# Two partial-sum buffers from the pooling path, and three operands loaded in place, in the last projection

## The chip, the core and the metric

The kernel runs on one core of one Trainium2 chip. The metric is the device time of one execution in microseconds (us). TensorE is called PE in the profile, VectorE DVE, ScalarE ACT, GpSimd POOL and SyncE SP; DMA transfers are issued by SP, in order, and each issue may first wait for semaphores. A wait at the head of SP's queue holds up every transfer that stands behind it.

## The reference, cut to what matters

Two layers work on 1024 latent tokens of 1024 channels (and 256 context tokens). The even layer runs a convolution branch and a gated linear recurrence side by side; the odd layer pools over windows, gates and projects back. The change touches only the end of the odd layer and the residual sum behind it:

```
z = h @ p["w_in"]
u, g = jnp.split(z, [W_POOL], axis=-1)
d = multiscale_pool(...)            # windows 2, 4, 8, 16 along rows of 64 tokens
y = einsum(d, w_grp) * scale
out = (y * silu(g)) @ p["w_out"]    # 2048 -> 1024 channels: the last projection
x = x + gate * out
return rmsnorm(x, final_g)
```

## The kernel before

Activations lie channels by tokens: a tile is 128 channels on the partitions by 1024 tokens, or one of its halves of 512. Products are taken in three passes for precision: each float32 operand is split into a high and a low part (`split`, lines 101 to 103: ACT casts the high part, DVE subtracts it for the low part), and PE multiplies high by high, high by low and low by high (`prod`, lines 931, 933 and 934). On top of this the large products use a Strassen-like scheme on 2 by 2 blocks with seven products: `quad` takes weights p1 to p7 and seven operands b11, t1, t2, b21, t3, b22 and t4, and sums into three PSUM tiles named qa, qb and qc. There are four PSUM tiles of 512 columns for this (`pm`), so the next quad can begin while one tile of the last one is still in use.

The last projection has 2048 input channels. It is computed in two halves of 1024 (part 0, names ending in `wo0`; part 1, `wo1`), and each half in four quads for the output rows m, m+1 with m = 0, 2, 4, 6. The last two quads of part 1 are written out apart (`last_half0`, names ending in `_l`). In the profile the buffer numbers are left out: `qa_wo`, `y_t3h`, `wq_wo` stand for all quads and both parts, and `h` and `l` at the end of an operand are its high and low part.

- **Operands.** The seven operands of each part lie in DRAM (`y_raw`). `y_operand` loads each as two tiles of 128 by 1024 into a raw tile (`yr_t...`, `yr_b...`, line 1350), and splits it into a high and a low tile. For b11, b21 and t4 these lie in `dpool`, for t1, t2, t3 and b22 in `d2pool`, which has 16 tiles: exactly the four such operands of one part, so that those of part 1 take over the tiles of part 0. The raw tiles come from `xpool` (8 tiles). For part 1, t3, b22 and t4 are loaded one after the other in the first quad of part 1 (line 1516), and use few raw tiles in turn.
- **Weights.** `wquad` loads two raw tiles (`wr_wo`, line 897; two buffers in all, so that the next quad's weights can be loaded only when the split of this quad's is through) and makes the seven weights (`ws_wo`, `wr_wo` sums at lines 911 to 919, `wq_wo` splits).
- **Partial sums.** For each quad of part 0, `put` loads a half row of the residual stream that the first layer left in DRAM (`xp` from `x1_part`, line 1472), adds the PSUM result times the gate (`gated`, line 1455, DVE) and stores it back (line 1481). The tile for it comes from `vpool`, which has two buffers of 512 columns. Each quad needs four such tiles: rows i = 0 and 1, halves h = 0 and 1. In part 1 the sums are loaded whole (`x` from `x1_part`, line 1503) and end in the final norm.
- **Two other buffers.** `apool` has two buffers of 640 columns (`atile`). The pooling path uses them for window sums; from the first quad of part 1 on they hold the two running sums of squares of the final norm (`fin`).
- **y sums.** `y_sums` (lines 883 to 886 in `block_sums`) forms the operands of part 1 from the last pair of rows, with a temporary tile `yt` from `vpool`, and stores them (line 1331). It is called within `put`.

A scheduler orders the instructions of each engine from the program and its own estimates, so that a change of buffers moves instructions on all of them.

Of the kernel before, what the change touches and what calls it, by code (L numbers as in the profile page):

```python
# [9 lines left out]
F32 = mybir.dt.float32  # L10
# [6 lines left out]
S = 1024  # L17
# [4 lines left out]
H = 512  # L22
# [29 lines left out]
BOPS = ("b11", "t1", "t2", "b21", "t3", "b22", "t4")  # L52
# [3 lines left out]
def body(ctx, tc, xT, ctxT, cc, ccol, modT, modW, win, gw, wout, wu, grp, wg, wo1, small, edge, ident, outT):  # L56
    nc = tc.nc
# [14 lines left out]
    y_raw = [{n: dram.tile([P, 2 * S], F32, tag=f"y_{n}_{p}", name=f"y_{n}_{p}") for n in BOPS} for p in range(2)]  # L72
# [5 lines left out]
    def xtile(name, dt=F32):  # L78
        return xpool.tile([P, S], dt, tag="x", name=name)

    def ttile(name):
        return tpool.tile([P, H], F32, tag="t", name=name)

    def atile(name):
        return apool.tile([P, NR * PW], F32, tag="acc", name=name)
# [15 lines left out]
    def split(src, hi, lo, eng):  # L101
        return (nc.scalar.copy(hi, src),  # L102
                eng.tensor_tensor(out=lo, in0=src, in1=hi.bitcast(F32), op=sub))  # L103
# [194 lines left out]
    with ExitStack() as sctx:  # L298
# [12 lines left out]
        def raw_tile(name):  # L311
            tag = ("wr", "wh", "wl")[raws[0] % 3]
            raws[0] += 1
            return wpool.tile([P, D], F32, tag=tag, name=name)
# [310 lines left out]
    with ExitStack() as actx:  # L625
# [88 lines left out]
        for j in range(KT):  # L714
# [20 lines left out]
            name = "gb0" if final else f"xb{j + 1}"  # L735
# [6 lines left out]
            if state is None:  # L742
                for m in range(2 * KT, 3 * KT):
                    part = L[m % 6][:, :D]
# [20 lines left out]
            name = "gb1" if final else f"vg{j + 1}"  # L765
# [79 lines left out]
        lo = wpool.tile([P, D], F32R, tag="wl", name="wl_gb4")  # L845
# [18 lines left out]
    def vtile(name):  # L864
        return vpool.tile([P, H], F32, tag="v", name=name)
# [16 lines left out]
    def block_sums(b11, b12, b21, b22, t3, eng):  # L882
        eng.tensor_tensor(out=t3, in0=b22, in1=b12, op=sub)
        eng.tensor_tensor(out=b12, in0=b12, in1=b11, op=sub)
        eng.tensor_tensor(out=b11, in0=b22, in1=b12, op=sub)
        eng.tensor_tensor(out=b21, in0=b21, in1=b11, op=sub)
        return dict(t2=b11, t1=b12, t3=t3, t4=b21, b22=b22)
# [54 lines left out]
    def quad(w, name, ops, put, ahead=None):  # L942
        p1, p2, p3, p4, p5, p6, p7 = w
        a, c, b = psum(f"qa_{name}"), psum(f"qc_{name}"), psum(f"qb_{name}")
        prod(a, p1, ops["b11"], True, False)
        with tc.high_priority(offset=EVAC):
            evac = nc.scalar.copy(b, a)
        prod(c, p5, ops["t1"], True, False)
        with tc.high_priority(offset=EVAC):
            put(1, 1, c, 0)  # L950
        prod(b, p6, ops["t2"], False, False)
        with tc.high_priority(offset=EVAC):
            put(0, 1, b, 0)
        prod(a, p2, ops["b21"], False, True)
        with tc.high_priority(offset=EVAC):
            put(0, 0, a, None)
        w = None
        if ahead is not None:
            with tc.issue_after(evac.ins):
                w = ahead()  # L960
        prod(b, p7, ops["t3"], False, False)
        with tc.high_priority(offset=EVAC):
            put(1, 1, b, 1)
        prod(c, p3, ops["b22"], False, True)
        with tc.high_priority(offset=EVAC):
            put(0, 1, c, 1)
        prod(b, p4, ops["t4"], False, True)
        with tc.high_priority(offset=EVAC):
            put(1, 0, b, None)
        return w  # L970


    def keep_part(parts, name, i, x):
        parts[i] = ttile(f"s{i}_{name}")
        nc.scalar.copy(parts[i], x)
# [6 lines left out]
    def gated(n, between):  # L982
        th, tl = d2tile(f"ybh{n}", F32R), d2tile(f"ybl{n}", F32R)
        for h in range(2):
            y = vtile(f"yr{n}_{h}")
            nc.sync.dma_start(y, yb_raw[n][:, HALF[h]])
            vec(nc.vector.tensor_tensor, out=y, in0=y, in1=sbs[n][h], op=mult)
            cast(th[:, HALF[h]], y)
            gp(out=tl[:, HALF[h]], in0=y, in1=th[:, HALF[h]].bitcast(F32), op=sub)
            fill(between)  # L990
        bh.append(th)
        bl.append(tl)
# [277 lines left out]
    for i in range(KH):  # L1270
# [3 lines left out]
        t = block_sums(b11, b12, b21, b22, ttile(f"xt3_{i}"), nc.vector)  # L1274
# [66 lines left out]
    def y_sums(m):  # L1341
        t = block_sums(*y_blocks(m), vtile(f"yt3_{m}"), nc.vector)
        for name in ("t1", "t2", "t3", "t4"):
            y_store(m, name, t[name])

    def y_operand(ops, part, name, raw_tile, alloc):
        hi, lo = [], []
        for q in range(2):
            r = raw_tile(f"yr_{part}_{name}_{q}")
            nc.sync.dma_start(r, y_raw[part][name][:, q * S : (q + 1) * S])  # L1350
            hi.append(alloc(f"y{part}_{name}h{q}", F32R))
            lo.append(alloc(f"y{part}_{name}l{q}", F32R))
            split(r, hi[q], lo[q], nc.vector)
        halves = lambda ts: [t[:, h] for t in ts for h in HALF]
        ops[name] = halves(hi), halves(lo)
# [3 lines left out]
    def y_operands(part, raws, names=BOPS, alloc=None):  # L1359
        for name in names:  # L1360
            y_operand(yops[part], part, name, next(raws),
                      alloc or (dtile if name in ("b11", "b21", "t4") else d2tile))
# [11 lines left out]
    def wo1_weights(part, m):  # L1374
        return wquad([wo1[m + i, part] for i in range(2)], f"wo{part}_{m}", wo1_ring,
                     part == 1 and m >= KT - 4)
# [69 lines left out]
    def square_fin(m, h, cols, v):  # L1446
        first = fin[h] is None
        if first:
            fin[h] = atile(f"fin{h}")
        square_acc(fin[h][:, cols], v, first, f"fq{m}_{h}_{cols.start}")  # L1450
        if m in GAINED:
            nc.scalar.activation(v, v, AF.Identity, scale=col(O_FG + m))
# [6 lines left out]
    def copied(name, x):  # L1459
        t = ttile(f"b_{name}")  # L1460
        nc.scalar.copy(t, x)
        return t

    for m in range(0, KT, 2):
        parts = {}

        def put(i, h, x, part):
            if part == 0:
                keep_part(parts, f"wo0_{m}", i, x)
                return  # L1470
            t = vtile(f"xp{m}_{i}_{h}")
            nc.sync.dma_start(t, x1_part[m + i][:, HALF[h]])
            if part == 1:

                if i == 1:
                    x = copied(f"wo0_{m}", x)
                s = x if i == 0 else parts[i]
                nc.vector.tensor_tensor(out=s, in0=x, in1=parts[i], op=add)
                x = s
            gated(m + i, t, x)  # L1480
            nc.sync.dma_start(x1_part[m + i][:, HALF[h]], t)
            if (m, i, h) == (0, 0, 1):
                y_sums(NK - 2)
        def nxt():
            if m < KT - 2:
                with tc.issue_after(stored[0].ins):
                    return wo1_weights(0, m + 2)
            w = wo1_weights(1, 0)
            y_operands(1, iter([xtile]), BOPS[3:4])
            return w  # L1490

        if m == KT - 2:
            with tc.issue_after(loaded[0].ins):
                y_operands(1, iter([xtile] * 2), BOPS[1:3])
        w = quad(w, f"wo0_{m}", yops[0], put, nxt)
        if m == 2:
            with tc.issue_after(loaded[0].ins):
                y_operands(1, iter([xtile]), BOPS[:1], lambda name, dt: xtile(name, dt))
    def x2_load(m):
        with tc.issue_after(loaded[0].ins):  # L1500
            for k in (m, m + 1):
                x1[k] = (xtile if k < KH else dtile)(f"x2_{k}")
                nc.sync.dma_start(x1[k], x1_part[k])

    x2_load(0)
    for m in range(0, KT - 4, 2):
        def put(i, h, x, part):
            v = x1[m + i][:, HALF[h]]
            if i == 1 and part == 1:
                x = copied(f"wo1_{m}", x)  # L1510
            gated(m + i, v, x)
            if part != 0:
                square_fin(m + i, h, slice(0, H), v)
        def ahead():
            if m == 0:
                y_operands(1, iter([xtile] * 3), BOPS[4:])
            w = wo1_weights(1, m + 2)
            x2_load(m + 2)
            return w

        w = quad(w, f"wo1_{m}", yops[1], put, ahead)
# [97 lines left out]
    m = KT - 4  # L1619
    wa = w  # L1620
    wb, _, _ = last_half0(m, wa, ahead)
# [140 lines left out]
```

## Time and profile before

| | |
|---|---|
| median of three runs | 1331.81 us (1330.71 to 1332.05) |
| profiled execution | 1331.6 us, of which 1329.8 us are the span from the first to the last instruction |
| PE busy | 1282.6 us, 96% of the span |
| DVE busy | 1139.7 us, 86% |
| ACT busy | 631.0 us, 47% |
| last projection | from 1142 us to about 1312 us of the span |

All times below are microseconds from the start of the span. In a row of the timeline the first number is the start, the second the duration (matmuls overlap, so the distance of two starts is what one costs), then engine, line, operation, tiles; in brackets the idle time of the engine just before it and what ended it. A row of a table of windows has the stretch, its length, busy time and number of instructions of PE, PE's weight loads, DVE, ACT and POOL, the granted PE clock, the busy share of the DMA engines and GB/s. A row of waits has who waited, for what, total us, times and the longest. A row of transfers has what was moved, issuer, number, size and the median time from issue to landing.

### The profile page before, as it was taken

How to read it: one execution, taken by the hardware profiler on the slowest of the kernel's cores; microseconds unless marked ns; L12 is line 12 of the kernel's file. 1: busy time of each engine (PE TensorE's matmuls, PEld its weight loads, DVE VectorE, ACT ScalarE, POOL GpSimd, SP SyncE). 2: the span in 40 equal slices, each digit the busy share in tenths (PEclk: the TensorE clock that was granted, in tenths of full speed). 3: DMA queues.
4: the chain of work that ended last, by engine and by line, in shares of the span. 5: the costliest groups of instructions: out<-in, count | busy, mean ns of one | idle time of the engine just before them, and what ended most of it. 6: DMA issues, size and time to landing. Idle time of an engine off the chain costs nothing. (4 is left out here: it accounts for less than half of the span.)

```text
span 1329.8 us, 15728 instructions
## 1 busy us (share of the span) xinstructions
PE 1282.6 (96%) x5600; PEld 1026.3 (77%) x5600; DVE 1139.7 (86%) x1771; ACT 631.0 (47%) x919; POOL 320.6 (24%) x172
## 2 busy tenths in 40 slices
PE   8999999999999999969999999999999999999896
PEld 3468888888888887858887888788777888877684
DVE  7959999998999989998788758998899977966775
ACT  5433665566566533227325346643333434734442
POOL 2252644355444556523210032000000000000002
PEclk9999999999999999989998999999999999999997
DMA  9934111112111233522555356234333335767623
GB/s 360 345 117 145 56 55 49 56 56 72 40 64 51 100 107 125 172 96 80 167 190 182 120 192 188 88 127 151 118 112 111 117 113 166 261 222 256 214 100 127
DMA packets 82867, 181.80 MB, mean 137 GB/s; under 512 B 7778, under 2 KB 27618, under 8 KB 82788
## 3 DMA queue, kind: packets, MB, share of 16 engines
q1 hardware_dynamic: 74340, 176.60, 39.7%
q10 hardware_dynamic: 8448, 4.20, 1.1%
q8 instruction: 44, 0.72, 0.2%
q14 instruction: 35, 0.29, 0.1%
HBM read 136.72 MB, written 44.04 MB: 136 GB/s over the span
## 5 line engine op out<-in xcount | busy, mean ns | idle before, releaser
L475 DVE SCALAR_TENSOR_TENSOR conv<-u,sm,conv 128x505 f32<-128x505 f32 (+6 forms) x224 | 153.1, 746 | 0.8
L1582 POOL TENSOR_TENSOR o<-x,rr 128x256 f32<-128x256 f32 (+1 forms) x9 | 8.0, 927 | 460.6 <-ACT rr L1570 460.6
L475 ACT ACTIVATE l<-g,sm 128x512 f32<-128x512 f32 (+1 forms) x96 | 58.7, 619 | 57.8 <-PE g L475 56.0
L281 PE MATMUL fold<-graw,wu 128*128 128x512 f32 x128 | 57.4, 609 | 1.6 <-DMA wu<-wu 1.6
L475 POOL TENSOR_TENSOR l<-l,l 128x1280 f32<-128x1280 f32 x16 | 47.1, 2961 | 26.1 <-DVE conv L475 21.1
L475 PE MATMUL wob<-ybl,wh_wob 128*128 128x512 f32 x128 | 50.6, 395 | 2.4 <-POOL ybl L475 2.4
L475 PE MATMUL wob<-ybh,wh_wob 128*128 128x512 f32 x128 | 51.6, 403 | 0.0
L281 PEld LDWEIGHTS fold<-graw,wu 128*128 128x128 f32 x128 | 24.8, 195 | 33.5 <-issue 29.6
L475 PE MATMUL wob<-ybh,wl_wob 128*128 128x512 f32 x128 | 50.4, 394 | 0.0
L475 PE MATMUL gb<-h0l,wh_gb 128*128 128x512 f32 x128 | 49.8, 389 | 0.0
L475 PE MATMUL gb<-h0h,wh_gb 128*128 128x512 f32 x128 | 49.8, 389 | 0.0
L475 PE MATMUL vg<-h0h,wh_vg 128*128 128x512 f32 x128 | 49.8, 389 | 0.0
L475 PE MATMUL vg<-h0h,wl_vg 128*128 128x512 f32 x128 | 49.8, 389 | 0.0
L475 PE MATMUL vg<-h0l,wh_vg 128*128 128x512 f32 x128 | 49.8, 389 | 0.0
L475 PE MATMUL va<-h0h,wh_va 128*128 128x512 f32 x128 | 49.8, 389 | 0.0
L475 PE MATMUL va<-h0l,wh_va 128*128 128x512 f32 x128 | 49.8, 389 | 0.0
L475 PE MATMUL va<-h0h,wl_va 128*128 128x512 f32 x128 | 49.8, 389 | 0.0
L475 PE MATMUL gb<-h0h,wl_gb 128*128 128x512 f32 x128 | 49.8, 389 | 0.0
L102 ACT CAST wq_g<-wr_g 128x512 fp32r<-128x512 f32 x48 | 28.2, 620 | 45.1 <-DVE wr_g L912 18.3
L475 DVE TENSOR_TENSOR_SCAN l<-l,l 128x256 f32<-128x256 f32 (+1 forms) x32 | 48.7, 1521 | 1.1
L102 ACT CAST wq_wo<-wr_wo 128x512 fp32r<-128x512 f32 x48 | 28.9, 620 | 40.5 <-DMA wr_wo<-wo 13.8
L475 DVE SCALAR_TENSOR_TENSOR conv<-cL,wsum,conv 128x506 f32<-128x506 f32 (+3 forms) x70 | 47.6, 746 | 0.2
(591 smaller groups left out, 4303.2 us busy)
## 6 DMA issues: line engine op xcount, KB each, us to landing
mod<-modT SPq DMA_DIRECT2D x20, 512.0 KB, 6.7
x_part<-xp SPq DMA_DIRECT2D x32, 256.0 KB, 2.6
mod<-modT SPq DMA_DIRECT2D x32, 256.0 KB, 3.2
wr_v<-wfold SPq DMA_DIRECT2D x16, 512.0 KB, 4.1
wr_g<-wg SPq DMA_DIRECT2D x16, 512.0 KB, 4.4
wr_wo<-wo SPq DMA_DIRECT2D x16, 512.0 KB, 4.6
yr_t<-y_t SPq DMA_DIRECT2D x16, 512.0 KB, 5.7
y_b<-y SPq DMA_DIRECT2D x24, 256.0 KB, 3.8
```

The lines of the kernel that those rows point to most:

```text
L102: return (nc.scalar.copy(hi, src), eng.tensor_tensor(out=lo, in0=src, in1=hi.bitcast(F32), op=sub))
L281: nc.tensor.matmul(ps, w[:, kc], gs[i], start=(i == 0), stop=(i == 3))
L475: last[eng] = f(*args, **kw)
L1582: nc.gpsimd.tensor_tensor(out=o[:, k - k0], in0=v, in1=rr, op=mult)
```

## The change

In part 0 the tiles for row i = 0 come from `apool`, those for i = 1 from `vpool` as before, so that four buffers stand where two did. For the last three operands of part 1 (t3, b22, t4) no raw tile is taken: the transfer goes into the low tile itself, ACT casts the high part from there, and DVE subtracts in place.

```diff
     def y_operand(ops, part, name, raw_tile, alloc):
         hi, lo = [], []
         for q in range(2):
-            r = raw_tile(f"yr_{part}_{name}_{q}")
-            nc.sync.dma_start(r, y_raw[part][name][:, q * S : (q + 1) * S])
+            if raw_tile is not None:
+                r = raw_tile(f"yr_{part}_{name}_{q}")
+                nc.sync.dma_start(r, y_raw[part][name][:, q * S : (q + 1) * S])
             hi.append(alloc(f"y{part}_{name}h{q}", F32R))
             lo.append(alloc(f"y{part}_{name}l{q}", F32R))
+            if raw_tile is None:
+                r = lo[q].bitcast(F32)
+                nc.sync.dma_start(r, y_raw[part][name][:, q * S : (q + 1) * S])
             split(r, hi[q], lo[q], nc.vector)
...
-            t = vtile(f"xp{m}_{i}_{h}")
+            t = vtile(f"xp{m}_{i}_{h}") if i else atile(f"xp{m}_{i}_{h}")[:, :H]
             nc.sync.dma_start(t, x1_part[m + i][:, HALF[h]])
...
         def ahead():
             if m == 0:
-                y_operands(1, iter([xtile] * 3), BOPS[4:])
+                y_operands(1, iter([None] * 3), BOPS[4:])
             w = wo1_weights(1, m + 2)
             x2_load(m + 2)
             return w
```

The order of the instructions moves as follows at three places. The number behind a name is that of the tile; `x_part_107` to `114` are the rows 0 to 7 of the sums in DRAM, and `xp_i_h` is the tile of row i, half h.

First, SP's queue during the second quad of part 0, from the sums of the first quad to the weights of the third (`wr_wo_4`). Before:

```order
L1472 DMA xp_0_1_9208<-x_part_107 128x512
L1481 DMA x_part_108<-xp_1_1_9189 128x512
L1481 DMA x_part_107<-xp_0_1_9208 128x512
L1331 DMA y_t_1_104<-yt_14_9213 128x512
L1472 DMA xp_1_0_9234<-x_part_108 128x512
L1331 DMA y_t_1_101<-y_8849 128x512
L1472 DMA xp_0_0_9294<-x_part_109 128x512
L1331 DMA y_t_1_102<-y_8849 128x512
L1331 DMA y_t_1_106<-y_8850 128x512
L897 DMA wr_wo_4_0_9298<-wo 128x1024
L1481 DMA x_part_108<-xp_1_0_9234 128x512
L897 DMA wr_wo_4_1_9300<-wo 128x1024
```

And in the change:

```order
L1485 DMA x_part_107<-xp_0_0_9143 128x512
L1476 DMA xp_0_0_9294<-x_part_109 128x512
L1485 DMA x_part_108<-xp_1_1_9189 128x512
L1485 DMA x_part_108<-xp_1_0_9234 128x512
L1476 DMA xp_1_1_9340<-x_part_110 128x512
L1476 DMA xp_1_0_9376<-x_part_110 128x512
L1485 DMA x_part_107<-xp_0_1_9208 128x512
L897 DMA wr_wo_4_0_9298<-wo 128x1024
L1476 DMA xp_0_1_9359<-x_part_109 128x512
L897 DMA wr_wo_4_1_9300<-wo 128x1024
```

The sums of the second quad (rows 109 and 110) are now loaded a quad ahead, in front of the third quad's weights; each such load still waits for the store that frees its tile. The four `y_sums` stores (line 1331) have left this stretch: they stand earlier.

Second, DVE around the first quad of part 0, from the weight p7 of that quad to the first weight of the next. Before:

```order
L103 TENSOR_TENSOR wq_wo_0_7_8992<-ws_wo_0_8979,wq_wo_0_7_8992 128x512
L103 TENSOR_TENSOR wq_wo_0_4_8999<-wr_wo_0_1_8974,wq_wo_0_4_8999 128x512
L1440 SCALAR_TENSOR_TENSOR y_8850<-vp_6546,sm,y_8850 128x512
L103 TENSOR_TENSOR y_t3l_9047<-yr_t_0_9044,y_t3h_9046 128x1024
L103 TENSOR_TENSOR y_t3l_9053<-yr_t_1_9050,y_t3h_9052 128x1024
L103 TENSOR_TENSOR wq_wo_0_3_8996<-wr_wo_0_0_8972,wq_wo_0_3_8996 128x512
```

And in the change:

```order
L103 TENSOR_TENSOR wq_wo_0_7_8992<-ws_wo_0_8979,wq_wo_0_7_8992 128x512
L883 TENSOR_TENSOR yt_14_9213<-y_8850,y_8849 128x512
L103 TENSOR_TENSOR wq_wo_0_4_8999<-wr_wo_0_1_8974,wq_wo_0_4_8999 128x512
L1444 SCALAR_TENSOR_TENSOR y_8850<-vp_6546,sm,y_8850 128x512
L884 TENSOR_TENSOR y_8849<-y_8849 128x512
L103 TENSOR_TENSOR y_t3l_9047<-yr_t_0_9044,y_t3h_9046 128x1024
L103 TENSOR_TENSOR y_t3l_9053<-yr_t_1_9050,y_t3h_9052 128x1024
L885 TENSOR_TENSOR y_8849<-y_8850,y_8849 128x512
L103 TENSOR_TENSOR y_t4l_9071<-yr_t_0_9068,y_t4h_9070 128x1024
L103 TENSOR_TENSOR wq_wo_0_3_8996<-wr_wo_0_0_8972,wq_wo_0_3_8996 128x512
```

Three y sums and one operand split now come before the split of the weight p3, the last reader of a raw weight tile.

Third, SP's queue where the last three operands of part 1 are loaded. Before:

```order
L897 DMA wr_wo_2_0_9809<-wo 128x1024
L897 DMA wr_wo_2_1_9811<-wo 128x1024
L1481 DMA x_part_113<-xp_0_1_9691 128x512
L1350 DMA yr_t_0_9773<-y_t_1_104 128x1024
L1350 DMA yr_t_1_9779<-y_t_1_104 128x1024
L1472 DMA xp_1_0_9708<-x_part_114 128x512
L1481 DMA x_part_114<-xp_1_1_9672 128x512
L1350 DMA yr_b_0_9785<-y_b_1_105 128x1024
L1481 DMA x_part_114<-xp_1_0_9708 128x512
L1350 DMA yr_b_1_9791<-y_b_1_105 128x1024
L1350 DMA yr_t_0_9797<-y_t_1_106 128x1024
L1350 DMA yr_t_1_9803<-y_t_1_106 128x1024
```

And in the change, where the first tile of t3 (`y_t3l_9774`) stands three rows ahead of these:

```order
L897 DMA wr_wo_2_0_9803<-wo 128x1024
L897 DMA wr_wo_2_1_9805<-wo 128x1024
L1356 DMA y_t3l_9779<-y_t_1_104 128x1024
L1356 DMA y_t4l_9794<-y_t_1_106 128x1024
L1507 DMA x_2_9833<-x_part_109 128x1024
L1507 DMA x_3_9835<-x_part_110 128x1024
L1485 DMA x_part_114<-xp_1_1_9672 128x512
L1356 DMA y_b22l_9784<-y_b_1_105 128x1024
L1485 DMA x_part_114<-xp_1_0_9708 128x512
L1356 DMA y_t4l_9799<-y_t_1_106 128x1024
L1356 DMA y_b22l_9789<-y_b_1_105 128x1024
```

The loads of the sums (`xp`) have left this stretch, the operands go into their low tiles, and two whole rows of the sums (`x_2`, `x_3`) are loaded between them. In the program the loads of t3 and b22 wait for the matmuls of part 0 that last read the tile they go into, and none of the six waits for the split of another operand. On PE the same matmuls stand in another order: where the order before put the products with t3, b22 and t4 of part 1's first quad close together, the change has 16 matmuls of the second quad between the first half and the rest of the b22 product.

## The prediction

> **What bounds the kernel now.** I read the totals, then the last projection in windows of 10 us, then PE's timeline at each hole, then who was late there. The total:
>
> ```profile
> PE 1282.6 (96%) x5600; PEld 1026.3 (77%) x5600; DVE 1139.7 (86%) x1771; ACT 631.0 (47%) x919; POOL 320.6 (24%) x172
> ```
>
> PE is the bound, so what an edit is worth is the time in which PE stands still, and only 47 us of the span are left for that. In the last projection:
>
> ```profile
> 1170.00:1180.00 10.00, 10.00 (x46) 8.29 (x45) 4.62 (x8) 2.84 (x6) 0.00 (x0) 1.00 0.91 314
> ...
> 1190.00:1200.00 10.00, 6.51 (x29) 5.12 (x28) 3.87 (x7) 2.22 (x4) 0.00 (x0) 1.00 0.90 299
> 1200.00:1210.00 10.00, 10.00 (x39) 8.09 (x38) 6.26 (x11) 4.08 (x7) 0.00 (x0) 0.83 0.76 258
> ...
> 1230.00:1240.00 10.00, 9.59 (x41) 7.25 (x40) 7.74 (x10) 2.11 (x4) 0.00 (x0) 1.00 0.84 279
> 1240.00:1250.00 10.00, 8.10 (x31) 5.49 (x31) 7.77 (x11) 5.15 (x8) 0.00 (x0) 1.00 0.56 184
> 1250.00:1260.00 10.00, 8.43 (x34) 6.23 (x35) 7.06 (x10) 5.96 (x9) 0.00 (x0) 1.00 0.60 181
> ```
>
> A full window has 46 matmuls. Two places fall short: 29 and 39 at 1190 to 1210, and 41, 31 and 34 at 1230 to 1260. The first on PE:
>
> ```profile
> 1194.10 0.39 PE L931 MATMUL qa_wo<-y_b21h,wq_wo 128*128 128x512 f32 x1
> ...
> 1195.23 0.39 PE L934 MATMUL qa_wo<-y_b21h,wq_wo 128*128 128x512 f32 x1
> 1199.11 0.47 PE L931 MATMUL qa_wo<-y_b11h,wq_wo 128*128 128x512 f32 x1 [3.49 <-DVE xp L1455]
> ...
> 1200.68 0.63 PE L931 MATMUL qa_wo<-y_b11h,wq_wo 128*128 128x512 f32 x1
> ...
> 1203.96 0.40 PE L934 MATMUL qc_wo<-y_b22h,wq_wo 128*128 128x512 f32 x1
> ```
>
> Five matmuls from 1194.10 to 1195.23 give 0.227 us each. From 1195.23 to 1203.96 the trace has 15 matmuls, worth 15 x 0.227 = 3.40 us, and took 8.73: **5.3 us lost**. 3.65 of these are the wait (1199.11 less 1195.23 less 0.23), 1.68 the slower matmuls behind it: the eight from 1200.68 to 1203.96 stand 0.41 apart, and the window's granted clock is 0.83. PE waited for a PSUM tile that DVE had not yet read:
>
> ```profile
> 1198.21 0.75 DVE L1455 SCALAR_TENSOR_TENSOR xp<-qb_wo,m,xp 128x512 f32<-128x512 f32 x1 [4.09 <-issue]
> ```
>
> And DVE waited for the sum's load, which stood on SP behind the stores that free the two tiles (the two `wr_wo` rows are used below):
>
> ```profile
> 1172.39 0.46 SPq L897 DMA_DIRECT2D wr_wo<-wo  x1
> ...
> 1187.79 0.33 SPq L897 DMA_DIRECT2D wr_wo<-wo  x1
> 1188.45 0.98 SPq L1481 DMA_DIRECT2D x_part<-xp x2
> ...
> 1193.37 0.32 SPq L1472 DMA_DIRECT2D xp<-x_part  x1
> ...
> 1194.27 0.38 SPq L1472 DMA_DIRECT2D xp<-x_part  x1
> ```
>
> A store lands in 4.4 us, the next load in 4.0 more:
>
> ```profile
> wr_wo<-wo SPq DMA_DIRECT2D x12, 512.0 KB, 4.6
> yr_t<-y_t SPq DMA_DIRECT2D x11, 512.0 KB, 6.1
> ...
> x_part<-xp SPq DMA_DIRECT2D x16, 256.0 KB, 4.4
> xp<-x_part SPq DMA_DIRECT2D x14, 256.0 KB, 4.0
> ```
>
> The second place is the first quad of part 1:
>
> ```profile
> 1239.09 0.50 PE L931 MATMUL qb_wo<-y_t3h,wq_wo 128*128 128x512 f32 x1
> 1240.35 0.50 PE L933 MATMUL qb_wo<-y_t3l,wq_wo 128*128 128x512 f32 x1 [0.76 <-DVE y_t3l L103]
> ...
> 1249.89 0.50 PE L933 MATMUL qc_wo<-y_b22l,wq_wo 128*128 128x512 f32 x1 [0.76 <-DVE y_b22l L103]
> ...
> 1253.42 0.50 PE L933 MATMUL qb_wo<-y_t4l,wq_wo 128*128 128x512 f32 x1 [0.75 <-DVE y_t4l L103]
> ...
> 1255.01 0.40 PE L931 MATMUL qc_wo<-y_t1h,wq_wo 128*128 128x512 f32 x1
> ```
>
> The order has 43 matmuls from the first to the last of these starts: 43 x 0.227 = 9.8 us of work in 15.9, **6.1 us lost**. All wait for the split of t3, b22 or t4, and these for their loads:
>
> ```profile
> 1232.01 1.46 SPq L1350 DMA_DIRECT2D yr_t<-y_t  x2
> ...
> 1240.32 0.32 SPq L1350 DMA_DIRECT2D yr_b<-y_b  x1
> ```
>
> ```profile
> 1237.99 1.05 ACT L102 CAST y_t3h<-yr_t 128x1024 fp32r<-128x1024 f32 x1 [7.89 <-DMA yr_t<-y_t]
> ```
>
> ```profile
> 1239.07 1.22 DVE L103 TENSOR_TENSOR y_t3l<-yr_t,y_t3h 128x1024 fp32r<-128x1024 f32 x1 [2.16 <-ACT y_t3h L102]
> ```
>
> The b22 load leaves 1.3 us after the t3 split begins (1239.07): the loads pass through raw tiles one pair after the other, load, cast, subtract.
>
> **The change part by part.** *Four buffers for the sums.* The work is the same: as many loads, stores and DVE operations of the same size. In the new order the loads for a quad stand a quad ahead. Two points on PE, which the new order reaches after as many matmuls:
>
> ```profile
> 1167.24 0.39 PE L931 MATMUL qb_wo<-y_t2h,wq_wo 128*128 128x512 f32 x1
> ...
> 1183.95 0.50 PE L931 MATMUL qb_wo<-y_t4h,wq_wo 128*128 128x512 f32 x1 [0.22 <-ACT b_wo L1461]
> ```
>
> The sum that came late is that of the second quad's t4 product, which begins at 1183.95 and ends 12 matmuls later, at 1186.7. Its load now leaves once the store behind the first quad's t4 product has landed. In the new order that product ends 15 matmuls ahead of 1167.24, at 1163.8; with DVE the store leaves near 1166, lands by 1171, and the load by 1175. That is over 10 us of cover, so the wait for the PSUM tile goes, and the slow matmuls with it: **-5.3 us**. Next at that place would be the fourth quad's weights. Their issue hangs on DVE's split of the third quad's, not on the sums: it left at 1187.79, and 4.6 us later, at 1192.4, it has landed, against a use after 1195.
>
> *In-place operands.* Count from T, the last b22 matmul of part 0. By the new order PE comes to the second tile of t3 88 matmuls later (20.0 us), to the first of b22 after 94 (21.3), to its second after 116 (26.3), to t4 after 122 (27.7). Before:
>
> ```profile
> 1225.06 0.39 PE L934 MATMUL qc_wo<-y_b22h,wq_wo 128*128 128x512 f32 x1
> ```
>
> ```profile
> 1228.37 0.94 SPq L897 DMA_DIRECT2D wr_wo<-wo  x2
> ```
>
> So the weights ahead of the operands left 3.3 us after T. In the new order more DVE work stands before them, and I take T+5. The first t3 tile goes before. Behind the weights stand seven more transfers of 512 KB and two of 256 KB; with the weights 5.2 MB, which at the 314 GB/s of the window 1170 to 1180 (DMA share 0.91) need 16.7 us. A cast and a subtraction (1.05 and 1.22) follow. The second t3 tile is third in line: T+5 + 5.0 + about 3 + 2.3 = T+15 against 20.0, ample. b22's first tile is seventh: 3.9 MB, 12.5 us, so T+5 + 12.5 + 1 + 2.3 = T+20.8 against 21.3: on time with nothing to spare. b22's last is at T+25 against 26.3. Between no wait and the bound by bandwidth with a late start of 3 us, this leaves 0 to 3 us; I keep **1 us** and count **-6.1 + 1.0**. DVE does the subtraction in place in the same 1.22 us, as far as the rows go: the same sizes and types.
>
> *What the new order adds.* The split of p3 frees the raw tile for `wr_wo_2_1`:
>
> ```profile
> 1154.98 0.33 SPq L897 DMA_DIRECT2D wr_wo<-wo  x1
> ```
>
> ```profile
> 1156.00 1.22 DVE L103 TENSOR_TENSOR y_t4l<-yr_t,y_t4h 128x1024 fp32r<-128x1024 f32 x1
> ...
> 1169.21 0.68 DVE L884 TENSOR_TENSOR y<-y 128x512 f32<-128x512 f32 x1
> ```
>
> Three y sums (0.68 each) and one t4 split (1.22) ahead of it delay it by at most 3.3 us, to 1158.3. It lands at 1162.9 (4.6); then seven DVE operations of 0.68 to the low part of p5, 1167.7. PE, which began t2 at 1167.24, now begins t1 there and needs that low part at its third matmul, 1167.7. It is just on time; with a landing of 6 us it is 1.4 late. I take **+0.5**, bounds 0 and 2. The y sums were off PE's path where they stood and are so here; their stores leave earlier. Short waits for ACT's copies out of PSUM stay. The one at 1183.95 waited 0.22 us and cost about 0.4. In the new order PE reaches the t4 products of the later quads sooner after t3, with more casts ahead of the copy on ACT: one or two more such waits, **+0.7**, bounds 0 and 2.
>
> The sum: -5.3 - 6.1 + 1.0 + 0.5 + 0.7 = -9.2 us. From the profiled execution's 1331.6 that is 1322.4; its median lies 0.2 higher, so **1322.6**. If no new wait comes, -11.4, 1320.4; with all bounds reached (3 + 2 + 2), -4.4, 1327.4.
>
> A rule bears on the price of left-over waits. The row: a wait of 3.49 us was followed by matmuls 0.41 apart for 3.3 us, waits of 0.8 us (1249.89, 1253.42) by none so slow. The Trainium skill (TensorE: Matmul & The Clock Gate, What's actually happening) says that the gate halves the clock only after an idle window of about 3.4 us and opens after as long a busy one; the trace agrees. By it left-over waits cost themselves alone, 1322.6; if every wait drew slow matmuls in proportion (1.68 to 3.65), the 2.2 us kept would cost 1.0 more, 1323.6.
>
> **The rivals.** *The operands bunch.* The six loads no longer wait for each other, but all but one stand behind two weights loads that wait for DVE, and share the DMA engines with two whole rows of sums. If the weights leave at T+8 and the transfers run at the 258 to 279 GB/s of the windows 1200 and 1230 (5.2 MB in 19.4 us, 2.7 more), b22 and t4 are 4 to 6 us late, and the second gain is gone while the first stays: -5.3 - 6.1 + 6 + 1.2 = -4.2, 1327.6. For it: DMA shares of 0.76 to 0.90 while DVE and SP, too, are busy; against it: the loads leave 10 us sooner relative to their use. [...]
>
> *The weights fall behind in SP's queue: slower.* Sums loaded ahead each wait for a store to land, and the third quad's weights stand behind three such loads, the last two close before them:
>
> ```profile
> SPq L1472 <- DMA x_part<-xp: 19.0, 9, 4.4
> ```
>
> These weights left at 1172.39 before. I expect the same: landed at 1177.0, split at 1178.3, used 12 matmuls ahead of 1183.95, at 1180.8 without its wait: 2.5 us of slack. If the loads ahead hold SP for the longest wait, 4.4 us, and 0.4 more, PE waits 2.3 us; if the same holds for three more quads, and one wait is long enough for the slow clock (+1.7), it is 4 x 2.3 + 1.7 = 10.9; with the 1.2 us and the operands half late (3) 15.1 against 11.4 saved: 1335.5. It decides once the delay exceeds the slack by 2 us in each of four quads. Against it: the nine waits took 2.1 us on average, and the stores are of a quad earlier.
>
> *Nothing is won*: one place goes and the weights cost half of that rival: within 2 us of 1331.8. That the change doesn't do what it says is excluded by the order: the loads stand where the tiles let them.
>
> **How the numbers follow.** Forecast 0.68, bunched operands 0.18, nothing won 0.07, weights behind 0.07. Two in ten left out: the range reaches from 1319.0 (all saved, the short waits of today too) to 1328.5. A difference below 0.2% (2.7 us) can't be told from none here. Faster by more than that is below 1329.1, which the first two hold: 0.87; same 0.07; slower 0.06.
>
> **What would show it.** In the profile after: no wait of PE for `xp` above 1 us and no window with a clock of 0.83 before the tail; row-1 loads issued some 10 us before their DVE operation; six loads from SP into `y_t3l`, `y_t4l`, `y_b22l` within 15 us; waits for these splits below 1.5 us in sum; the span shorter by 8 to 11. I am wrong if PE waits for `wq_wo`, or for b22 and t4 by several us.

## The result and the profile after

The change takes 1321.65 us, median of four runs (1319.1 to 1322.99), against 1331.8 for the kernel before (four runs, 1330.71 to 1332.05): a ratio of 0.9923, interval 0.9906 to 0.994. Two later timings of the change, beside other kernels, gave 0.9932 (0.9912 to 0.9953) and 0.9936 (0.9915 to 0.9957). The forecast was 1322.6. The profiled execution has a span of 1320.6 us, 9.2 less than before.

The windows of the last projection, with the columns of the windows of before (PE, weight loads, DVE, ACT, POOL, granted clock, DMA share, GB/s):

```profile
1150.00:1160.00 10.00, 8.66 (x38) 6.63 (x36) 10.00 (x14) 8.50 (x13) 0.00 (x0) 1.00 1.00 347
...
1190.00:1200.00 10.00, 10.00 (x46) 8.29 (x45) 7.23 (x13) 4.08 (x7) 0.00 (x0) 1.00 0.94 308
1200.00:1210.00 10.00, 10.00 (x46) 8.29 (x45) 5.82 (x10) 2.20 (x4) 0.00 (x0) 1.00 0.76 259
...
1220.00:1230.00 10.00, 10.00 (x46) 8.28 (x45) 10.00 (x14) 6.31 (x9) 0.00 (x0) 1.00 0.95 360
1230.00:1240.00 10.00, 10.00 (x46) 8.29 (x45) 8.62 (x13) 4.84 (x7) 0.00 (x0) 1.00 0.99 376
1240.00:1250.00 10.00, 10.00 (x46) 8.29 (x45) 8.25 (x12) 7.19 (x12) 0.00 (x0) 1.00 0.32 99
```

Both short places are full, at a clock of 1.00. What is short now is 1150 to 1160 and a little ahead of it. All that PE still waits for between 1138 and 1302 in this execution:

```profile
PE qb_g L931 <- ACT y L1410: 0.9, 1, 0.9
PE qb_wo L931 <- ACT s_wo L975: 0.9, 1, 0.9
PE qc_wo L931 <- ACT y_b22h L102: 0.4, 1, 0.4
```

All three stand in the hand-over, where the gate's last product and the first quad of the last projection overlap:

```profile
1145.58 0.39 PE L934 MATMUL qa_wo<-y_b11h,wq_wo 128*128 128x512 f32 x1
1146.91 0.50 PE L931 MATMUL qb_g<-x_t4h,wq_g 128*128 128x512 f32 x1 [0.94 <-ACT y L1410]
...
1157.71 0.39 PE L934 MATMUL qa_wo<-y_b21h,wq_wo 128*128 128x512 f32 x1
1158.51 0.49 PE L931 MATMUL qc_wo<-y_b22h,wq_wo 128*128 128x512 f32 x1 [0.41 <-ACT y_b22h L102]
1159.93 0.50 PE L931 MATMUL qb_wo<-y_t3h,wq_wo 128*128 128x512 f32 x1 [0.93 <-ACT s_wo L975]
```

For all kernels below I count holes in one way: where two neighbouring matmuls start more than 0.27 us apart, what exceeds 0.227 is lost. By this count PE lost 13.1 us from 1136 to 1301 in the profile of before, and 3.1 in that of the change. That is 10.0 less; the span shows 9.2, mainly since the change's execution was 0.9 us later already at 1030, where both kernels had run the same instructions.

**How the sums run now.** SP's queue from the second quad's last weights to the third quad's, and the two operations on DVE that use the loads of 1169.89:

```profile
1159.54 0.33 SPq L897 DMA_DIRECT2D wr_wo<-wo  x1
...
1169.89 1.12 SPq L1476 DMA_DIRECT2D xp<-x_part  x2
...
1173.16 0.33 SPq L897 DMA_DIRECT2D wr_wo<-wo  x1
...
1175.55 0.33 SPq L897 DMA_DIRECT2D wr_wo<-wo  x1
```

```profile
1190.72 0.75 DVE L1459 SCALAR_TENSOR_TENSOR xp<-s_wo,m,xp 128x512 f32<-128x512 f32 x1
1191.38 0.75 DVE L1459 SCALAR_TENSOR_TENSOR xp<-qb_wo,m,xp 128x512 f32<-128x512 f32 x1
```

The loads that came last in the profile of before, just ahead of the PSUM tile that PE wanted, leave 20.8 us ahead of their use.

**How the operands run now.** The first and the last of the six loads on SP:

```profile
1218.74 0.32 SPq L1356 DMA_DIRECT2D y_t3l<-y_t  x1
...
1232.06 0.32 SPq L1356 DMA_DIRECT2D y_b22l<-y_b  x1
```

The transfers from 1142 to 1252 (name, issuer, number, size, median from issue to landing), then the last of the first b22 tile on DVE, and PE's first use of it:

```profile
y_t3l<-y_t SPq DMA_DIRECT2D x2, 512.0 KB, 6.8
...
y_t4l<-y_t SPq DMA_DIRECT2D x2, 512.0 KB, 9.0
y_b22l<-y_b SPq DMA_DIRECT2D x2, 512.0 KB, 9.6
```

```profile
1239.50 1.23 DVE L103 TENSOR_TENSOR y_b22l<-y_b22l,y_b22h 128x1024 fp32r<-128x1024 f32 x1
```

```profile
1241.67 0.39 PE L933 MATMUL qc_wo<-y_b22l,wq_wo 128*128 128x512 f32 x1
```

Each transfer takes longer than the 6.1 us of before, at a DMA share of 0.99, and still is in time: b22's first tile with 1241.67 less 1240.73 = 0.94 us to spare.

### The profile page after: what moved, and what is told of

It reads as the page before. It is cut to its first block, busy times and chain, and to the rows that moved or that the text cites. A ratio compares the mean times of both kernels' runs of the same rounds, so it can differ in the third digit from the quotient of the medians.

```text
span 1320.6 us, 15724 instructions
## 1 busy us (share of the span) xinstructions
PE 1278.6 (97%) x5600; PEld 1026.3 (78%) x5600; DVE 1139.3 (86%) x1771; ACT 630.7 (48%) x919; POOL 320.5 (24%) x172
## 5 line engine op out<-in xcount | busy, mean ns | idle before, releaser
L475 POOL TENSOR_TENSOR l<-l,uc 128x1280 f32<-128x1280 f32 x16 | 47.2, 2970 | 0.0
```

Of the source, the lines that this page charges most:

```text
L475: last[eng] = f(*args, **kw)
```

## The experiments

The table has the holes of each kernel in its profile, in three stretches: the hand-over (1136 to 1162), the rest of the first half (to 1215, where the first hole of before was) and the second half (to 1301, where the second was), then the time against the kernel before on the same chip, with its interval.

| kernel | hand-over | first half | second half | ratio |
|---|---|---|---|---|
| before | 0.5 | 6.3 | 6.2 | |
| before, second profile | 3.0 | 3.6 | 5.4 | 0.999 (0.9971 to 1.0008) |
| the change | 3.1 | 0 | 0 | 0.9923 (0.9906 to 0.994) |
| the change, second profile | 2.6 | 0 | 1.1 | 0.9932 (0.9912 to 0.9953) |
| the change, third profile | 2.8 | 0.4 | 0.7 | 0.9936 (0.9915 to 0.9957) |
| sums alone | 5.4 | 0.4 | 4.8 | 0.9959 (0.9944 to 0.9973) |
| operands alone | 2.7 | 7.1 | 1.5 | 0.9962 (0.9946 to 0.9977) |
| only t3 in place | 4.8 | 0 | 1.8 | 0.995 (0.9934 to 0.9965) |
| row 0 from the second quad on | 2.4 | 0.5 | 8.0 | 0.9982 (0.9966 to 0.9999) |
| loads behind the operands | 3.1 | 6.7 | 0 | 0.9956 (0.994 to 0.9971) |
| one load ahead | 4.7 | 2.8 | 2.1 | 0.9945 (0.9926 to 0.9963) |
| first half's t3, b22, t4 in place too | 4.4 | 1.4 | 3.3 | 0.9977 (0.9961 to 0.9993) |
| first half's b21 in place too | 5.4 | 0 | 1.7 | 0.9932 (0.9916 to 0.9948) |
| first half's t2 and b21 in place too | 4.5 | 1.1 | 3.7 | 0.994 (0.9925 to 0.9955) |

### Each part alone

The four buffers without the operands in place:

```diff
-                y_operands(1, iter([None] * 3), BOPS[4:])
+                y_operands(1, iter([xtile] * 3), BOPS[4:])
```

> The four buffers for the sums alone; the last three operands pass through raw tiles as before. Theory A (two gains that are independent of each other, and one price that belongs to the buffers): the hole at 1195 to 1204 is gone (-5.3 us), that at 1239 to 1255 stays (6 us), and the new short waits at 1146 to 1160 are there (2.4 us more than before), since two loads of the sums stand ahead of the two of b21 on SP: 1331.8 - 5.3 + 2.4 = 1329. Theory B (the gain comes from the changed order of PE's products and needs both parts): both holes shrink or both stay; within 2 us of 1331.8 with a hole left at 1195, or below 1326 with the hole at 1239 gone too.

The operands in place without the four buffers:

```diff
-            t = vtile(f"xp{m}_{i}_{h}") if i else atile(f"xp{m}_{i}_{h}")[:, :H]
+            t = vtile(f"xp{m}_{i}_{h}")
```

> The operands in place alone; all four sums of a quad share two buffers as before. Theory A: the hole at 1239 to 1255 is gone (-6.1 us), that at 1195 to 1204 stays with its wait of some 3.5 us and slow matmuls behind it, no new waits at 1146 to 1160: 1331.8 - 6.1 = 1325.7. Theory B: the loads of the sums, which still wait for stores, stand among the operands' loads on SP and hold them up; b22 and t4 are late, 2 to 6 us of waits are left there, 1328 to 1332.

Measured: 0.9959 and 0.9962. From 1331.8 that is 5.5 and 5.1 us, 10.5 together, against 8.5 to 10.3 of the change in its three timings: within the intervals the parts add up. What PE waits for with the sums alone, from 1160 to 1302:

```profile
PE qb_wo L931 <- ACT b_wo L1465: 0.9, 1, 0.9
PE qb_wo L933 <- DVE y_t4l L103: 0.8, 1, 0.8
PE qc_wo L933 <- DVE y_b22l L103: 0.8, 1, 0.8
PE qb_wo L931 <- ACT y_t4h L102: 0.7, 1, 0.7
```

And PE with the operands alone, at the first place:

```profile
1195.30 0.39 PE L934 MATMUL qa_wo<-y_b21h,wq_wo 128*128 128x512 f32 x1
1199.05 0.76 PE L931 MATMUL qa_wo<-y_b11h,wq_wo 128*128 128x512 f32 x1 [3.36 <-DVE xp L1459]
```

With the sums alone the wait for `xp` is gone and those for b22 and t4 stay; with the operands alone it is the other way round. This is theory A in the main. One thing was not foreseen, and it has something of B: with the sums alone the second place shrinks too, and t3 is not waited for at all. Its loads do not leave sooner, 7.2 us after the last b22 matmul of part 0 (1225.78 less 1218.54) against 7.0 before (1232.01 less 1225.06). PE asks for it later: it begins t3 as the 83rd matmul after that one, 20.0 us behind it, where it began as the 61st, 14.0 us behind it, before. So this part of the gain is one of PE's order, which moved with the buffers. The kernel with the operands alone keeps t3 at the 61st matmul, and there the loads in place, 0.9 us ahead of that b22 matmul and 2.0 us behind it, remove the wait by themselves.

### Only t3 in place

```diff
-                y_operands(1, iter([None] * 3), BOPS[4:])
+                y_operands(1, iter([None, xtile, xtile]), BOPS[4:])
```

> As the change, but of the last three operands only t3 is loaded in place; b22 and t4 pass through raw tiles. Theory E (the wait was a shortage of raw tiles, so two fewer users cure most of it): the waits for b22 and t4 at 1240 to 1250 are 1.5 us or less. Theory F (each operand in place saves its own wait): b22 and t4 wait as with the buffers alone, where these waits made 3.7 us, and the time is 3 to 4 us above that of the change.

Between 1160 and 1302 PE waits for no split of b22 or t4:

```profile
PE qb_wo L931 <- ACT wq_wo L102: 0.5, 1, 0.5
PE qb_wo L931 <- ACT b_wo L1465: 0.3, 1, 0.3
```

The holes of the second half are 1.8 us, against 4.8 with none in place: theory E, a shortage of raw tiles that two users fewer cure. The ratio, 0.995, is 1.4 to 2.7 thousandths above that of the change; in the profile most of this difference stands in the hand-over (4.8 us), which the edit doesn't touch. What b22 and t4 in place add at their own place is 0.7 to 1.8 us (1.8 less the 0 to 1.1 of the change's three profiles), and whether the time shows it is open.

### The hand-over

The three waits there were new to me. Theory A was that the sums' first two loads cause them. Of SP's queue, first before, then in the change:

```profile
1134.73 2.37 SPq L1350 DMA_DIRECT2D yr_b<-y_b  x2
...
1143.32 2.25 SPq L1350 DMA_DIRECT2D yr_b<-y_b  x2
```

```profile
1135.20 0.92 SPq L1476 DMA_DIRECT2D xp<-x_part  x2
1136.22 1.66 SPq L1351 DMA_DIRECT2D yr_b<-y_b  x2
...
1146.13 1.04 SPq L1351 DMA_DIRECT2D yr_b<-y_b  x2
```

The two loads go ahead of b21's, and b22's leave 2.8 us later, of which 0.9 is the later execution. On ACT, which works in order, b21's and b22's casts stand ahead of the copies out of PSUM that PE waits for. Theory C: the y sums, 2 us of DVE work that moved ahead, do it. Two edits tell them apart. The first quad's row 0 from the pool of two again, so that the y sums come late, while two loads (now of the second quad) still stand ahead of b21:

```diff
-            t = vtile(f"xp{m}_{i}_{h}") if i else atile(f"xp{m}_{i}_{h}")[:, :H]
+            t = vtile(f"xp{m}_{i}_{h}") if i or m == 0 else atile(f"xp{m}_{i}_{h}")[:, :H]
```

> As the change, but the first quad's row 0 takes its tiles from the pool of two as before, so that the y sums on DVE come late again, while two loads of the sums (now of the second quad) still stand ahead of b21's two loads on SP. Theory A (the short waits at 1146 to 1160 come from the loads ahead of b21, which make b21's casts late on ACT and, behind them, the copy that PE waits for): the waits stay, 1321.7, at most 1 us off. Theory C (they come from the y sums, 2 us of DVE work that moved ahead): the waits are gone, 1319.2.

And the first two loads behind the operands (`yload` is the operands' last load):

```diff
-            nc.sync.dma_start(t, x1_part[m + i][:, HALF[h]])
+            if m == 0 and i == 0:
+                with tc.issue_after(yload[0].ins):
+                    nc.sync.dma_start(t, x1_part[m + i][:, HALF[h]])
+            else:
+                nc.sync.dma_start(t, x1_part[m + i][:, HALF[h]])
```

> As the change, with one edit: the first quad's two loads of row 0 are issued after the last load of the first half's operands, so behind b21, t3, b22 and t4 on SP. Buffers and y sums are those of the change. Theory A: b21's casts are 1 to 2 us earlier, the waits at 1146 to 1160 fall from 2.9 to 0.5 us: 1321.7 - 2.4 = 1319.2. Theory C: the waits stay, 1321.7.

With late y sums the two waits at b22 stayed (1.9 us, as in the change's first profile), so C falls for these. With the loads behind, the hand-over still lost 3.1 us, so A did not get what it foretold either; and both kernels lost more further on. A second profile of the kernel before bears on how much of it belongs to the change:

> The kernel before, with a second profile. The three profiles of the change have 2.6 to 3.0 us of holes at 1138 to 1162 where the one profile of before has 0.55, and 0 to 1.1 us from 1160 to the tail where it has 12.4. Theory A (the hand-over of the change is dearer by the two loads of the sums): again 0.5 to 1.2 us there. Rival C (the hand-over varies with the pace of the part ahead of it, whatever the kernel): 2 us or more. Both: again 11 to 13 us from 1160 to the tail, with the waits for the tile that xp holds and for the splits of t3, b22 and t4.

It lost 3.0 us in the hand-over, where its first profile lost 0.5. That is what one kernel shows from one execution to another. A wait for `s_wo` is in neither profile of before and in all three of the change (at least 0.7 us of holes), one for b22's cast in the change's first profile alone, and one for the copy of line 1406 or 1410 in all five.

Three more executions can be laid beside these. Up to the hand-over the kernels with the sums alone and with only t3 in place have the change's order on every engine, and that with the operands alone has the order of before. So the order of before lost 0.5, 3.0 and 2.7 us there, that of the change 3.1, 2.6, 2.8, 5.4 (of which 1.6 are slow clock behind a wait of 2.70) and 4.8: a mean of 2.1 against 3.7, with ranges that overlap. In the change's order the execution counts for much: the two that reached the gate's t4 product earliest, at 1027.2 and 1028.7, lost 5.4 and 4.8, and the three at 1031.4 to 1033.1 lost 2.6 to 3.1. A price of the change of some 1.7 us at this place is likely but not shown, and its cause stays open. The second profile also puts the first place of before in another light: PE waited 1.81 us there and not 3.49, and no slow matmuls followed.

Two further attempts at the hand-over, one load ahead in place of two (`loaded` is the last weights load), and b21 of the first half in place so that it leaves some ten transfers earlier:

```diff
+            if m == 0 and i == 0:
+                with tc.issue_after(loaded[0].ins):
+                    nc.sync.dma_start(t, x1_part[m + i][:, HALF[h]])
```

> As the change, but the first quad's row-0 loads of the sums are issued after the second quad's first weights, as far as the scheduler keeps that: one of them stands ahead of b21's loads on SP, the other moves behind the operands. Theory A: b21 leaves 0.5 us earlier and lands about 1 us earlier; the wait of 1.7 us at 1157 to 1160 shrinks to about 0.8; otherwise as the change: 0.9 us less, 0.9915 of before. Theory C (the y sums cause it): as the change. Rival D: new holes of several us further on, 0.994 to 0.997.

```diff
-            y_operands(0, iter([dtile] + [xtile] * (4 - 1)), BOPS[:4])
+            y_operands(0, iter([dtile, xtile, xtile, None]), BOPS[:4])
```

> As the change, with the first half's b21 loaded in place too. Its loads need no raw tile, so on SP they stand some ten transfers earlier, ahead of the sums' two loads, and t3's and b22's raw tiles no longer wait for b21's split; behind that the queue is the change's. Theory A: the wait for the copy of line 1410 is 0.6 us or less (no b21 cast waits for a load ahead of it on ACT) and that at 1157 to 1160 is gone, holes of 0.5 to 1 us where the change has 2.6 to 3.0: 2 to 2.5 us below the change, 0.9905 to 0.9915 of before. Rival C (the hand-over is late for another reason, the y sums or the pace of PE before it): as the change. Rival D: PE is 2 us earlier at the second quad and meets weights or casts that are not: the gain comes back as holes at 1165 to 1190.

With one load ahead the hand-over was 4.7 us. With b21 in place the wait for line 1410 was as foretold, but b22's cast was late by more:

```profile
1143.33 0.50 PE L931 MATMUL qb_g<-x_t4h,wq_g 128*128 128x512 f32 x1 [0.51 <-ACT y L1410]
...
1156.99 0.49 PE L931 MATMUL qc_wo<-y_b22h,wq_wo 128*128 128x512 f32 x1 [2.44 <-ACT y_b22h L102]
```

0.9932 cannot be told from the change beside it (0.9936). With t2 in place as well (the list reads `[dtile, xtile, None, None]`):

> As the kernel with b21 in place, with t2 of the first half in place too: two raw tiles more. In the order t2's loads stay behind the sums' two loads. Theory A: nothing is left to be won at the hand-over, so the same time as with b21 alone, within 1 us. Theory C: as the change.

0.994, the same within the interval; the wait for line 1410 was 2.6 us again. And with the first half's t3, b22 and t4 in place (`y_operands(0, iter([None] * 7), BOPS[4:])`):

> As the change, with the first half's t3, b22 and t4 loaded in place too, so that their loads no longer wait for a raw tile that b21's split frees. Theory A: t3's second tile leaves at about 1137 and not 1146; b22's tiles come free only as PE ends the part before, so that b22 is later than now; PE's order changes with it. If t4 comes ahead of b22 on PE, the 1.7 us at 1157 to 1160 are gone and the time is 1.7 us below the change; if PE waits for b22, 2 to 4 us above it. Rival D: holes further on.

0.9977: PE waited 1.6 us for `s_wo` and 0.9 for b22 in the first quad, and 1.9 for a copy in the second half. In this stretch a faster load of one operand only brought another to the front, and none of these is a better kernel than the change.

### How near the edge the queue runs

The kernel with the loads behind and the one with row 0 from the second quad on show what the change has been spared. In the former, SP's store, the load of an operand of the second half that stands behind it, ACT's cast that waits for this load, the copy behind the cast, and PE:

```profile
1182.43 0.32 SPq L1491 DMA_DIRECT2D x_part<-xp  x1
1182.80 0.43 SPq L1353 DMA_DIRECT2D yr_b<-y_b  x1
```

```profile
1187.13 1.04 ACT L102 CAST y_b11h<-yr_b 128x1024 fp32r<-128x1024 f32 x1 [1.74 <-DMA yr_b<-y_b]
1188.08 0.58 ACT L1467 COPY b_wo<-qb_wo 128x512 f32<-128x512 f32 x1
```

```profile
1188.71 0.50 PE L931 MATMUL qb_wo<-y_t4h,wq_wo 128*128 128x512 f32 x1 [3.10 <-ACT b_wo L1467]
```

In the latter:

```profile
1218.73 0.32 SPq L1476 DMA_DIRECT2D xp<-x_part  x1
...
1220.10 0.89 SPq L1356 DMA_DIRECT2D y_t3l<-y_t  x2
```

```profile
1226.95 1.04 ACT L102 CAST y_t3h<-y_t3l 128x1024 fp32r<-128x1024 f32 x1 [8.17 <-DMA y_t3l<-y_t]
1227.90 1.04 ACT L102 CAST y_b21h<-yr_b 128x1024 fp32r<-128x1024 f32 x1
```

```profile
1228.99 0.80 PE L931 MATMUL qa_wo<-y_b21h,wq_wo 128*128 128x512 f32 x1 [4.86 <-ACT y_b21h L102]
```

t3's cast waits for a load that left late, and b21's cast, whose data are there, stands behind it. In the kernel with the loads behind, the operand's load left 2.5 us later than in the change (1182.80 against 1180.30). With slow matmuls behind the waits these two places lost 5.0 and 8.0 us. Rival D for the change itself, that its first profile was a lucky execution, was tried twice:

> The change again, with a second profile. Theory A: no wait of PE from 1160 to 1302, as in the first profile, and again about 1.7 us at 1157 to 1160 behind the cast of b22 and the copy s_wo; the wait for the copy of line 1410 anywhere from 0.4 to 3 us, since it varied so in kernels that are alike up to there; 0.990 to 0.994 of before. Rival D (the first profile was a lucky execution: with so little slack a load that lands 1 to 2 us later opens holes of 3 to 8 us, as in the two kernels with small edits of the queue): holes of that size at other places, and a ratio near 0.996.

> The change, timed beside the two kernels above. Theory A and the sum of the two parts: 0.992 to 0.9935 of before, holes of 3 to 4 us in the last projection ahead of the tail. Rival D: a third profile with other holes, above 6 us.

It falls: 3.7 and 3.9 us of holes in all, of which 1.1 us in each lie behind the hand-over, at short waits of the kind that the prediction allowed for. The one in the first of the two:

```profile
1226.65 0.50 PE L931 MATMUL qb_wo<-y_t4h,wq_wo 128*128 128x512 f32 x1 [0.79 <-ACT b_wo L1465]
```

## Why the prediction was right, and where its steps were off

- **Sums, -5.3.** The mechanism held: no wait for `xp` above 1 us is left, and the part alone takes the first half from 3.6 or 6.3 us of holes to 0.4. The size was that of one execution. Its 5.3 us held 1.68 of slow clock that the second profile of before doesn't have; there the wait and its neighbour cost 2.0. A mean of both is 3.7 at this place.
- **Operands, -6.1 + 1.0.** The six loads leave within 13.3 us (1218.74 to 1232.06), and PE waits for no split. The 1.0 that I kept for b22's first tile was not lost, and the margin, put at 0.5 us in the working, was 0.94. The step that failed is the attribution: I gave the whole 6.1 to the operands. Sums alone took 0.6 to 1.4 of it, through PE's order, and t3 alone in place 3.0 more.
- **The late weight, +0.5.** `wr_wo_2_1` left at 1159.54, later than the 1158.3 I allowed, and PE did not wait, since it was itself 3.5 us later than I had put it, at 1170.72 and not 1167.24. With the loads behind the operands, PE came earlier and lost 1.7 us there: the mechanism is real, the term was nought here.
- **Copies out of PSUM, +0.7.** 0, 1.1 and 1.1 us in the three profiles: sized rightly.
- **The term that was missing** is the hand-over: 2.6 to 3.1 us in the change, 0.5 and 3.0 before. I had looked at SP's queue from the second quad on, and not at the two loads ahead of b21 in it. As to the sum it took the place of the 1.0 and the 0.5, which were not needed: the total of -9.2 came out (-8.5 to -10.3) by terms of which two were wrong in place. That they made up for each other is luck; that both long waits went is not.
- **The rivals.** The bunched operands did not decide: the share reached 0.95 to 0.99, above the 0.90 and 0.91 of the windows of before that I went by, but at 360 to 376 GB/s, where I had priced 258 to 279 (and 314 in the forecast). The Trainium skill (DMA: Bandwidth & Descriptors, Issuing engines are not separate DMA queues) says that all issues share the same 16 DMA engines and interleave; the trace agrees (landing 9.0 to 9.6 us), and b22's 0.94 us show how little was left. The weights did not fall behind: they left at 1173.16 and 1175.55, the first 0.8 us after that of before, with no wait of PE for `wq_wo`.

## What to carry to other kernels

A stall of several microseconds on a tile that DVE has not read may be a store, a load and a buffer two steps away: count how long before its use each load could leave, and give the buffers where that is shortest. Where an in-order engine casts loaded data and also empties PSUM, each cast that waits for a load is a wait of PE in waiting, so a load that leaves 2 us later can cost 5. And a hole read from one execution is a sample: two profiles of the same kernel gave 5.3 and 2.0 us at one place, so profile twice before pricing it.

## What the runs showed of the hardware that was not expected

- **Whether the slow clock follows a wait depends on where the wait falls.** Two waits of the same length, of the kernel with t2 and b21 in place and of the second profile of before, each with two windows:

```profile
1229.51 0.50 PE L931 MATMUL qb_wo<-y_t4h,wq_wo 128*128 128x512 f32 x1 [1.80 <-ACT b_wo L1465]
```

```profile
1227.35:1230.76 3.41, 1.61 (x7) 1.05 (x6) 3.41 (x6) 3.41 (x6) 0.00 (x0) 1.00 0.94 345
1230.76:1234.17 3.41, 3.41 (x9) 2.63 (x8) 3.39 (x5) 1.23 (x3) 0.00 (x0) 0.50 0.94 348
```

```profile
1200.57 0.47 PE L931 MATMUL qa_wo<-y_b11h,wq_wo 128*128 128x512 f32 x1 [1.81 <-DVE xp L1455]
```

```profile
1195.79:1199.20 3.41, 2.98 (x14) 2.12 (x12) 0.34 (x1) 1.07 (x2) 0.00 (x0) 1.00 0.73 269
1199.20:1202.61 3.41, 2.04 (x9) 1.72 (x10) 2.10 (x4) 0.82 (x2) 0.00 (x0) 1.00 0.95 330
```

  After the first, the clock is granted at 0.50 from 1230.76 to 1234.17, and matmuls stand 0.43 apart; this cost 1.6 us. After the second there is no slow matmul. In each of the fourteen profiles the slow stretches are 3.41 us long or a multiple of it (the last apart, which the end of the execution cuts off), and they begin whole multiples of 3.413 us apart, so they lie on one grid. The windows above are steps of this grid. The first wait lies whole in one step, in which PE is busy for 1.61 us; an edge at 1199.20 cuts the second into 0.43 and 1.37. Between 745 and 1300 us the profiles have 30 waits of PE above 1.2 us. All nine that have 1.73 us or more in one step were followed by a slow one, and none of the other 21, which have 1.65 at most; the longest of these, 2.45 us at 972, is cut into 1.06 and 1.39. The Trainium skill (TensorE: Matmul & The Clock Gate, What's actually happening) puts the gate's window at about 3.4 us and calls it free-running. The length and the grid agree; that it takes a whole idle window does not, as a step that was idle for half its length was enough. So the sentence of the prediction that left-over waits cost themselves alone holds here for waits below 1.7 us, and its wait of 3.49 us drew the slow clock with the 2.14 us that fell in one step (1196.97 to 1200.38).

- **The same instructions take 1026 to 1033 us.** Up to the gate's t4 product near 1030, all fourteen profiled executions ran the same instructions; it began at 1026.40 in the earliest and at 1033.13 in the latest. The holes that differ most are at 932 and 972, a wait for DVE of 1.4 to 2.5 us each in some executions (1.61 and 2.45 in the latest) and of less or nothing in others. Part of the spread of a kernel's times is made there, 170 us ahead of the change: of the 2.9 us between the spans of the change's three profiles, 1.8 were there at this product. Holes counted by stretch leave this part out.
